# A two-layer encoder on one core: the first feed-forward stage's down projection computed directly, and each stage's opening put in another order

## The chip, the core and the metric

The kernel runs on one core of a Trainium2 chip. The core has five engines that run their own instruction streams and wait for one another by semaphores: TensorE (PE, matmuls; its weight loads are listed apart as PEld), VectorE (DVE), ScalarE (ACT), GpSimd (POOL) and SyncE (SP). POOL and SP issue DMAs too. Matmul operands lie in SBUF, products in eight PSUM banks of 128 x 512 fp32. The metric is the device time of one execution in microseconds; the median of three runs is compared.

## What is computed

The input is 512 prompt tokens and 256 sample tokens, each of width 1024. Both go through the same trunk of two layers (the two batches never mix):

```python
for layer in range(2):
    x = x + 0.5 * swiglu(rms_norm(x, g[layer, 0]), w_gate, w_up, w_down)   # 1024 -> 2816 -> 1024
    hn = rms_norm(x, norm_mix[layer])
    if layer == 0: x = x + concat(s5(u), neighbourhood_attention(q, k, v)) @ w_out_even
    else:          x = x + windowed_gqa(q, k, v) @ w_out_odd
    x = x + 0.5 * swiglu(rms_norm(x, g[layer, 1]), w_gate, w_up, w_down)
return rms_norm(x, norm_final)
```

with `swiglu(x) = (silu(x @ w_gate) * (x @ w_up)) @ w_down`, all in fp32. There are four feed-forward (FFN) stages, q = 0 to 3, and they take most of the time. The S5 mixer of layer 0 is a diagonal state-space scan; it is run in chunks of 8 tokens, for which small matrices (W1, W2, E) are made from its parameters, two of 32 groups at a time.

## The kernel before

*Precision.* Each fp32 operand is split into a rounded high part (ACT's cast, `split`, L89) and a low part (VectorE's subtraction, L90); a product is three matmuls, high x high, high x low, low x high.

*Weights.* One generator, `weights`, fixes the order of all weight tiles. SP loads 128 x 1024 raw blocks into 7 buffers (`raw`, L80); a tile is then split into one of 7 `whl` buffers, four tiles ahead of use (`look`). Where PE is to take a sum of blocks, VectorE forms it in the raw buffers first.

*Gate and up.* The 768 tokens are two halves, 384 each; a pair b takes two of the 22 blocks of the hidden width (11 pairs). Gate and up of a pair each are a 2 x 2 block product computed with seven products instead of eight (Strassen-Winograd): `quad` has steps p1 to p7, one product each of 12 matmuls 128 x 384 (`prod`, L248). The weight sums s1 to s4 are VectorE's (L135 to L141), the token sums t1 to t4 are made once per stage.

*Down.* `down(b)` does the same for the down projection: seven steps of three tiles, 9 matmuls 128 x 512 per step (L354). Of the 21 tiles of results five are added to x by VectorE from PSUM (L358); the other sixteen are scaled into a buffer y by ACT (L361; five buffers) and added to x by an accumulating DMA on POOL's queue (L362). It needs four sums of weights (L114 to L119) and, made in `up`, four sums of h (L330 to L337). `woven` puts one down step after every second product of the next pair. The last pair's down projection is direct (`rows`, L411: 36 matmuls in rows of six) and is not part of this.

*The S5 matrices.* During the first stage, `s5_matrices` runs as a generator, one `next` after each step from b = 2 on. Each of its 16 turns: a chain of small POOL operations (`start`, L626 to L649) into w1, w2; then `finish`: W2d stored by POOL, four transposes of w1 on PE (L660), ACT's copy into w1e, 24 small matmuls on PE (L667 to L671), and two steps later `store`: W1d and Ed by POOL's DMA queue (L678, L679). The next `start` uses w1e as scratch (n1, n2 at L626), so it waits for W1d's DMA.

*A stage's opening.* The tokens' norm and transposes of the last two tiles, the sums t1 to t4 and their splits (`NormS.rest`, a generator: S1 minus S2 at L1263, t3's differences at L1277, the low halves by `lo`, L1226) are interleaved with the products of pairs 0 and 1. The token blocks "22" are held in raw buffers, which loads of weights wait for.

Of the kernel before, what the change touches and what calls it, by code (L numbers as in the profile page):

```python
# [16 lines left out]
ALU = mybir.AluOpType  # L17
# [3 lines left out]
P = 128  # L21
# [26 lines left out]
class Trunk:  # L48
# [49 lines left out]
    def weights(self):  # L98
# [26 lines left out]
        def quad(n, q, b):  # L125

            k = lambda z: (n, q, b, z)
            r1 = self.raw(self.a[n][q, 2 * b])
            a11, a12 = r1[:, :512], r1[:, 512:]
            yield k("11"), self.part(a11)  # L130
            yield k("12"), self.part(a12)
            r2 = self.raw(self.a[n][q, 2 * b + 1])
            a21, a22 = r2[:, :512], r2[:, 512:]
            s1 = self.wp.tile([P, 512], F32, tag="st", name="st", bufs=2)
            v.tensor_add(s1, a21, a22)  # L135
            v.tensor_sub(a21, a11, a21)
            v.tensor_sub(a11, s1, a11)
            yield k("s2"), self.part(a11)
            yield k("s1"), self.part(s1)
            yield k("s3"), self.part(a21)  # L140
            v.tensor_sub(a12, a12, a11)  # L141
            yield k("s4"), self.part(a12)
            yield k("22"), self.part(a22)

        def fast(q):
            both = ("w_gate", "w_up")
            first, second = ([quad(n, q, b) for n in both] for b in range(2))
            for z in first * 2 + second * 2 + first * 5:
                yield next(z)
            for b in range(1, NF // 2):  # L150
                pair = second if b == 1 else [quad(n, q, b) for n in both]
                yield from woven(b, chain(*pair), down(q, b - 1))
            for c in (NF - 2, NF - 1):
                yield from block("w_down", q, c)

# [69 lines left out]
    def ffn(self, q, norm, tail, extra=None):  # L225
# [5 lines left out]
        with ExitStack() as ctx:  # L231
# [5 lines left out]
            extra = extra(fp, room[:, 1, 2:].rearrange("p a n -> p (a n)")) if extra else iter(())  # L237

            def ct():
                return fp.tile([P, H], F32, tag="ct", name="ct", bufs=5)  # L240
# [10 lines left out]
            def quad(n, b, use):  # L251
# [16 lines left out]
                def p2():  # L268
                    o = bank()
                    prod(o, get("12"), "21", True)  # L270
                    v.tensor_add(z["p1"], o, z["p1"])
                    if b != 1:
                        use(0, 0, z["p1"])
# [13 lines left out]

                def p7():
                    prod(z["b"], get("s3"), "t3", False)
                    v.tensor_add(z["r5"], z["b"], z["r5"])  # L290
# [10 lines left out]

                return [p1, p2, p6, p5, p7, p3, p4]

# [6 lines left out]
            def up(b):  # L310

                last = b == NF // 2 - 1
                sums = {}
# [28 lines left out]
            def down(b):  # L342
# [4 lines left out]
                def step(h, w, bank, first, i, j):  # L347
# [19 lines left out]
                    ("s4", "22", "c", False, 0, 1))]  # L367

            def pair(b):
                return quad("w_gate", b, gate), quad("w_up", b, up(b))  # L370
# [4 lines left out]
            rest = norm.rest()  # L375
            for s in (norm.turn, g[0], u[0], norm.turn, g[1], u[1], g1[0], u1[0], g1[1], u1[1]):
                s()
# [6 lines left out]
            for b in range(1, NF // 2):  # L384
                g, u = (z[2:] for z in (g1, u1)) if b == 1 else pair(b)
                for s in woven(b, g + u, iter(down(b - 1))):
                    s()
# [4 lines left out]
            self.warm(at(1, 0)[:, 0:1])  # L392
            act = lambda f, i, n: hs[f"{n // 3 + 1}{f + 1}"][:, i, n % 3 * P : (n % 3 + 1) * P]
            for s in self.rows(act, q, tail):
                s()

    def rows(self, act, q, tail):

        nc = self.nc
        st = {}  # L400

        def step(n):
            t = TILES[n]
            if not st:
                st["t"] = tail()
                st["w"] = [[self.take("w_down", q, c, e) for e in range(2)] for c in (NF - 2, NF - 1)]
            for half in range(2):
                o = self.ps()
                for f, w in enumerate(st["w"]):
                    for j, i in ((0, 0), (1, 0), (0, 1)):  # L410
                        nc.tensor.matmul(o, act(f, i, n), w[half][:, j], start=f == 0 and (j, i) == (0, 0), stop=f == 1 and (j, i) == (0, 1))  # L411
                xs = self.x[t][:, half * 512 : (half + 1) * 512]
                nc.vector.scalar_tensor_tensor(xs, o, 0.5, xs, ALU.mult, ALU.add)
                if half == 0:
                    st["t"].before(t)
            st["t"].after(t)

        return [lambda n=n: step(n) for n in range(6)]

# [45 lines left out]
    def s5_matrices(self, pool, spare):  # L465
# [216 lines left out]
        for q in range(G // 2 + 1):  # L682
            if q:
                finish(q - 1)
                yield
# [524 lines left out]
class NormS(NormT):  # L1210
# [47 lines left out]
    def rest(self):  # L1258
# [3 lines left out]
        for n in range(3):  # L1262
            v.tensor_sub(s1[:, 3 + n], s1[:, 3 + n], s2[:, n])  # L1263
            self.lo("t2", n, s2[:, n])
        yield
        for n in range(3):
            self.lo("t1", n, s1[:, n])
        yield
# [11 lines left out]
        part("22", lambda n: self.C[n])  # L1280
        yield
        part("t4", lambda n: s1[:, 3 + n])
        yield
# [85 lines left out]
```

## Time and profile before

| | |
|---|---|
| runs, median (lowest to highest) | 2759.49 us (2758.82 to 2759.89) |
| the profiled execution | 2754.47 us, span 2752.7 us |
| PE busy | 2624.4 us, 95% of the span |
| DVE, ACT, POOL busy | 2072.1, 1661.6, 919.6 us |
| accumulating DMAs x<-y | 640 issues of 256 KB, 5.2 us to landing in the median |
| S5 stores W1d | 16 issues of 256 KB, 6.1 us in the median |

The span is the time between the first and the last record of that execution. Busy is what an engine's instructions took; matmuls are pipelined, so PE can be busy and still slow when its granted clock is low. The granted clock is given as a share of 2.4 GHz; its other level is 1.2 GHz.

### The profile page before, as it was taken

To read this page: it belongs to the slowest core of one execution; us is meant where nothing else is said; L and a number is where in the kernel's file an instruction comes from. 1 tells how busy PE (TensorE), PEld (TensorE's weight loads), DVE (VectorE), ACT (ScalarE), POOL (GpSimd) and SP (SyncE) were. 2 spreads that over 40 slices of the span, in tenths; PEclk is the share of its full clock that TensorE was granted. 3 is DMA by queue.
4 is the path that set the end of the run, shared out by engine and by line. 5 is a ranking of instruction groups with operands and counts; after the bars stand their busy time and mean duration, and the time that the engine had idled before them with its cause. 6 is when DMAs were issued, how large, how long until landed. Compare 5 with 4: busy or idle time off the path is not lost.

```text
span 2752.7 us, 40909 instructions
## 1 busy us (share of the span) xinstructions
PE 2624.4 (95%) x14276; PEld 2371.8 (86%) x14276; DVE 2072.1 (75%) x3982; ACT 1661.6 (60%) x3432; POOL 919.6 (33%) x1330
## 2 busy tenths in 40 slices
PE   6999999899899989999998999999999999999998
PEld 5987888788778789999997999999897778999997
DVE  7987776664585597787878887878737878787786
ACT  6654554454455566666666666666648766666665
POOL 0378877750380003333331233333200002333332
PEclk8999999899999999999999999999999999999999
DMA  3667676683626128877872778778501116787875
GB/s 140 131 166 155 138 167 138 140 189 96 136 83 180 59 80 192 172 161 162 169 167 66 174 162 172 161 169 169 153 16 55 39 47 155 171 173 170 171 162 132
DMA packets 172271, 381.22 MB, mean 138 GB/s; under 512 B 32960, under 2 KB 39744, under 8 KB 171808
## 3 DMA queue, kind: packets, MB, share of 16 engines
q0 software_dynamic: 96064, 178.89, 36.6%
q1 hardware_dynamic: 76000, 199.72, 23.0%
q8 instruction: 112, 1.84, 0.3%
q14 instruction: 95, 0.78, 0.1%
HBM read 194.97 MB, written 17.89 MB: 77 GB/s over the span
## 4 chain that ended last, share of the span: by engine, by line
PE 78%; POOL 6%; DVE 6%; DMA 5%; ACT 2%; issue 2%; SPq 0%; DVEq 0%; POOLq 0%; ACTq 0%
PE ps L248 39%; PE ps L354 18%; PE ps L222 8%; PE ps L436 4%; DMA W1d<-hct 3%; PE ps L411 2%; POOL x L362 1%; PE ps L1044 1%; DVE whl L90 1%; PE ps L1032 1%; PE ps L1197 1%; DMA x<-y 1%; DMA raw<-in_w_up 1%; PE ps L1063 1%; PE ps L827 1%
## 5 line engine op out<-in xcount | busy, mean ns | idle before, releaser
L362 POOL DMA_DIRECT2D x<-y x640 | 564.3, 1070 | 1166.7 <-ACT y L361 1032.4
L90 DVE TENSOR_TENSOR whl<-raw,whl 128x512 fp32r<-128x512 f32 x876 | 620.1, 713 | 400.3 <-ACT whl L89 388.7
L248 PE MATMUL ps<-bt,whl 128*128 128x384 f32 x4224 | 797.5, 341 | 48.6 <-ACT whl L89 41.0
L248 PEld LDWEIGHTS ps<-bt,whl 128*128 128x128 f32 x4224 | 758.3, 192 | 68.7 <-ACT whl L89 42.7
L89 ACT CAST whl<-raw 128x512 fp32r<-128x512 f32 x876 | 538.7, 620 | 282.3 <-PE ps L248 80.4
L248 PE MATMUL ps<-b,whl 128*128 128x384 f32 x3168 | 593.3, 339 | 1.2 <-DVE hct L317 1.2
L248 PEld LDWEIGHTS ps<-b,whl 128*128 128x128 f32 x3168 | 563.8, 190 | 12.1 <-DVE hct L317 1.6
L361 ACT ACTIVATE y<-ps 128x512 f32<-128x512 f32 x640 | 370.2, 597 | 107.6 <-DMA x<-y 54.5
L354 PE MATMUL ps<-whl,hl 128*128 128x512 f32 x1440 | 361.8, 395 | 0.3 <-ACT y L361 0.3
L354 PEld LDWEIGHTS ps<-whl,hl 128*128 128x128 f32 x1440 | 269.7, 189 | 50.5 <-ACT y L361 0.7
L354 PE MATMUL ps<-whl,h 128*128 128x512 f32 x1080 | 271.9, 395 | 6.4 <-ACT y L361 6.4
L354 PEld LDWEIGHTS ps<-whl,h 128*128 128x128 f32 x1080 | 201.2, 188 | 44.8 <-ACT y L361 8.2
L222 PE MATMUL ps<-hn,whl 128*128 128x256 f32 (+1 forms) x1248 | 229.9, 341 | 0.6 <-ACT hn L89 0.6
L222 PEld LDWEIGHTS ps<-hn,whl 128*128 128x128 f32 x1248 | 192.3, 191 | 29.0 <-issue 2.2
L358 DVE SCALAR_TENSOR_TENSOR x<-ps,x 128x512 f32<-128x512 f32 x200 | 132.8, 682 | 9.8 <-PE ps L354 9.6
L89 ACT CAST h<-hct 128x384 fp32r<-128x384 f32 x132 | 67.9, 514 | 114.5 <-DVE hct L317 114.3
L90 DVE TENSOR_TENSOR whl<-st,whl 128x512 fp32r<-128x512 f32 x128 | 92.1, 723 | 16.1 <-ACT whl L89 14.7
L436 PE MATMUL ps<-whl,ob 128*128 128x512 f32 x432 | 102.8, 392 | 0.0
L286 ACT COPY ct<-ps 128x384 f32<-128x384 f32 x88 | 42.4, 481 | 88.9 <-PE ps L248 88.9
L436 PEld LDWEIGHTS ps<-whl,ob 128*128 128x128 f32 x432 | 80.1, 188 | 18.4 <-issue 1.6
L199 POOL TENSOR_SCALAR ss<-ss 128x1 f32<-128x1 f32 x42 | 13.3, 318 | 243.1 <-ACT raw L198 240.3
L89 ACT CAST whl<-st 128x512 fp32r<-128x512 f32 x128 | 78.5, 617 | 19.3 <-PE ps L248 19.2
(255 smaller groups left out, 3364.7 us busy)
## 6 DMA issues: line engine op xcount, KB each, us to landing
x<-y POOLq DMA_DIRECT2D x640, 256.0 KB, 5.2
raw<-in_w_gate SPq DMA_DIRECT2D x88, 512.0 KB, 5.9
raw<-in_w_up SPq DMA_DIRECT2D x88, 512.0 KB, 3.8
raw<-in_w_down SPq DMA_DIRECT2D x88, 512.0 KB, 5.4
raw<-in_w_in_even SPq DMA_DIRECT2D x16, 512.0 KB, 4.3
raw<-in_w_in_odd SPq DMA_DIRECT2D x10, 512.0 KB, 6.9
W2d<-raw POOLq DMA_DIRECT2D x16, 256.0 KB, 2.4
W1d<-hct POOLq DMA_DIRECT2D x16, 256.0 KB, 6.1
```

The lines of the kernel that those rows point to most:

```text
L89: nc.scalar.copy(hl, src)
L90: nc.vector.tensor_sub(lo, src, hl.bitcast(F32))
L222: self.nc.tensor.matmul(o, w[k // 4][:, j, k % 4 * P : (k % 4 + 1) * P], act[i][k // 4][:, k % 4, k0 : k0 + n], start=k == 0 and (j, i) == ...
L248: nc.tensor.matmul(o, w[:, j, k * P : (k + 1) * P], B[z][:, i, k], start=first and k == 0 and (j, i) == (0, 0), stop=k == 3 and (j, i) == ...
L286: nc.scalar.copy(z["r5"], z["c"])
L354: nc.tensor.matmul(o, hs[h][:, c, n * P : (n + 1) * P], w[:, a], start=first and m == 0, stop=m == 2, skip_group_check=True)
L358: v.scalar_tensor_tensor(xs, o, 0.5, xs, ALU.mult, ALU.add)
L361: nc.scalar.activation(y, o, AF.Copy, scale=0.5)
L362: nc.gpsimd.dma_start(xs, y, accum_op=ALU.add)
L411: nc.tensor.matmul(o, act(f, i, n), w[half][:, j], start=f == 0 and (j, i) == (0, 0), stop=f == 1 and (j, i) == (0, 1))
L436: nc.tensor.matmul(o, act(i, k)[:, t * P : (t + 1) * P], st["w"][k][:, j], start=m == 0, stop=m == 11)
L827: nc.tensor.matmul(o[:, r, e], w1[:, (g2 + e) * 256 + r * P : (g2 + e) * 256 + (r + 1) * P], U[:, 16 * h + b + g2 + e], start=True, stop=True)
```

## The change

Three things are changed. In the first stage (q = 0) the down projection of pairs 0 to 9 is direct, as it was for the last pair alone: `plain`, twelve steps of 6 matmuls 128 x 512, each with one VectorE addition from PSUM into x; the h sums are left out (`last`), the weights are taken as they are, and the order of a pair is seven gate products, twelve short steps, seven up products. The S5 generator gets three more yields in front of `finish`, thirteen per turn. In the opening of every stage the first gate product stands before the norm's turn; p5 (plain sum s1) changes places with p6 (s2) for b = 0, `use(0, 0)` moves to p7; and in `NormS.rest` t1's low halves come first, and S1 minus S2 is put behind "22".

```diff
--- before.py
+++ after.py
@@ -133,14 +133,24 @@
             a21, a22 = r2[:, :512], r2[:, 512:]
             s1 = self.wp.tile([P, 512], F32, tag="st", name="st", bufs=2)
             v.tensor_add(s1, a21, a22)
+            if not b:
+                yield k("s1"), self.part(s1)
             v.tensor_sub(a21, a11, a21)
             v.tensor_sub(a11, s1, a11)
             yield k("s2"), self.part(a11)
-            yield k("s1"), self.part(s1)
+            if b:
+                yield k("s1"), self.part(s1)
             yield k("s3"), self.part(a21)
             v.tensor_sub(a12, a12, a11)
             yield k("s4"), self.part(a12)
             yield k("22"), self.part(a22)
+
+        def plain(q, b):
+
+            r = [self.raw(self.a["w_down"][q, 2 * b + f]) for f in range(2)]
+            for e in range(2):
+                for f in range(2):
+                    yield ("w_down", q, 2 * b + f, e), self.part(r[f][:, e * 512 : (e + 1) * 512])
 
         def fast(q):
             both = ("w_gate", "w_up")
@@ -149,9 +159,11 @@
                 yield next(z)
             for b in range(1, NF // 2):
                 pair = second if b == 1 else [quad(n, q, b) for n in both]
-                yield from woven(b, chain(*pair), down(q, b - 1))
-            for c in (NF - 2, NF - 1):
-                yield from block("w_down", q, c)
+                if q == 0:
+                    yield from chain(pair[0], plain(q, b - 1), pair[1])
+                else:
+                    yield from woven(b, chain(*pair), down(q, b - 1))
+            yield from plain(q, NF // 2 - 1)
 
         def out(n, kb, half):
             for e in range(2):
@@ -236,6 +248,8 @@
             hs = {z: h3[:, i] for i, z in enumerate(("11", "12", "22"))}
             extra = extra(fp, room[:, 1, 2:].rearrange("p a n -> p (a n)")) if extra else iter(())
 
+            act = lambda f, i, n: hs[f"{n // 3 + 1}{f + 1}"][:, i, n % 3 * P : (n % 3 + 1) * P]
+
             def ct():
                 return fp.tile([P, H], F32, tag="ct", name="ct", bufs=5)
 
@@ -269,7 +283,7 @@
                     o = bank()
                     prod(o, get("12"), "21", True)
                     v.tensor_add(z["p1"], o, z["p1"])
-                    if b != 1:
+                    if b > 1:
                         use(0, 0, z["p1"])
 
                 def p6():
@@ -286,6 +300,8 @@
                     nc.scalar.copy(z["r5"], z["c"])
 
                 def p7():
+                    if b == 0:
+                        use(0, 0, z["p1"])
                     prod(z["b"], get("s3"), "t3", False)
                     v.tensor_add(z["r5"], z["b"], z["r5"])
                     use(1, 1, z["r5"])
@@ -299,7 +315,7 @@
                     prod(z["b"], get("22"), "t4", False)
                     use(1, 0, z["b"])
 
-                return [p1, p2, p6, p5, p7, p3, p4]
+                return [p1, p2, p6, p5, p7, p3, p4] if b else [p1, p2, p5, p6, p7, p3, p4]
 
             def gate(f, t, o):
                 nc.scalar.activation(at(f, t), o, AF.Silu)
@@ -309,7 +325,7 @@
 
             def up(b):
 
-                last = b == NF // 2 - 1
+                last = b == NF // 2 - 1 or q == 0
                 sums = {}
 
                 def use(f, t, o):
@@ -366,6 +382,20 @@
                     ("22", "t4", "b", False, 1, 0), ("12", "21", "a", True, 0, 0), ("s1", "t1", "c", True, 1, 1),
                     ("s4", "22", "c", False, 0, 1))]
 
+            def plain(b):
+
+                st = {}
+
+                def step(e, n):
+                    if n == 0:
+                        st["w"] = [self.take("w_down", q, 2 * b + f, e) for f in range(2)]
+                    o = self.ps()
+                    self.rows(o, act, n, st["w"])
+                    xs = self.x[TILES[n]][:, e * 512 : (e + 1) * 512]
+                    v.scalar_tensor_tensor(xs, o, 0.5, xs, ALU.mult, ALU.add)
+
+                return [lambda e=e, n=n: step(e, n) for e in range(2) for n in range(6)]
+
             def pair(b):
                 return quad("w_gate", b, gate), quad("w_up", b, up(b))
 
@@ -373,7 +403,7 @@
             g1, u1 = pair(1)
             self.look = 4
             rest = norm.rest()
-            for s in (norm.turn, g[0], u[0], norm.turn, g[1], u[1], g1[0], u1[0], g1[1], u1[1]):
+            for s in (g[0], norm.turn, u[0], norm.turn, g[1], u[1], g1[0], u1[0], g1[1], u1[1]):
                 s()
             next(rest)
             for z in zip(g[2:], u[2:]):
@@ -383,39 +413,37 @@
                     s()
             for b in range(1, NF // 2):
                 g, u = (z[2:] for z in (g1, u1)) if b == 1 else pair(b)
-                for s in woven(b, g + u, iter(down(b - 1))):
+                for s in g + plain(b - 1) + u if q == 0 else woven(b, g + u, iter(down(b - 1))):
                     s()
                     if b > 1:
                         next(extra, None)
             for _ in extra:
                 pass
...
+    def rows(self, o, act, n, ww):
+
+        for f, w in enumerate(ww):
+            for j, i in ((0, 0), (1, 0), (0, 1)):
+                self.nc.tensor.matmul(o, act(f, i, n), w[:, j], start=f == 0 and (j, i) == (0, 0), stop=f == 1 and (j, i) == (0, 1))
...
@@ -681,6 +709,8 @@
         load(0)
         for q in range(G // 2 + 1):
             if q:
+                for _ in range(3):
+                    yield
                 finish(q - 1)
                 yield
                 yield
@@ -1260,11 +1290,10 @@
         v = self.k.nc.vector
         s1, s2 = self.S
         for n in range(3):
-            v.tensor_sub(s1[:, 3 + n], s1[:, 3 + n], s2[:, n])
+            self.lo("t1", n, s1[:, n])
+        yield
+        for n in range(3):
             self.lo("t2", n, s2[:, n])
-        yield
-        for n in range(3):
-            self.lo("t1", n, s1[:, n])
         yield
 
         def part(z, src):
@@ -1279,6 +1308,8 @@
         yield
         part("22", lambda n: self.C[n])
         yield
+        for n in range(3):
+            v.tensor_sub(s1[:, 3 + n], s1[:, 3 + n], s2[:, n])
         part("t4", lambda n: s1[:, 3 + n])
         yield
```

Three places in the order of instructions. First PE, in the first stage around the first S5 turn, before (ps: PSUM banks; b, bt: token blocks and sums; whl: split weights; h, hl: split hidden values; x9: nine alike in a row):

```order
L248 MATMUL ps<-bt_504,whl 128x384 x12
L248 MATMUL ps<-b_547,whl 128x384 x12
L660 MATMUL ps<-ident,raw 128x128 x4
L667 MATMUL ps<-raw,s5k 32x112 x2
L669 MATMUL ps<-s5k 32x16 x2
L671 MATMUL ps<-raw,s5k 32x112 x2
L667 MATMUL ps<-raw,s5k 32x112 x2
L669 MATMUL ps<-s5k 32x16 x2
L671 MATMUL ps<-raw,s5k 32x112 x2
L354 MATMUL ps<-whl,hl 128x512 x9
L248 MATMUL ps<-bt_598,whl 128x384 x12
```

And after the change, with the new line numbers (L262 product, L446 short step, L688 to L699 the turn):

```order
L262 MATMUL ps<-bt_594,whl 128x384 x12
L446 MATMUL ps<-whl,h_230 128x512 x12
L688 MATMUL ps<-ident,raw 128x128 x4
L695 MATMUL ps<-raw,s5k 32x112 x2
L697 MATMUL ps<-s5k 32x16 x2
L699 MATMUL ps<-raw,s5k 32x112 x2
L695 MATMUL ps<-raw,s5k 32x112 x2
L697 MATMUL ps<-s5k 32x16 x2
L699 MATMUL ps<-raw,s5k 32x112 x2
L446 MATMUL ps<-whl,h_230 128x512 x6
L446 MATMUL ps<-whl,hl 128x512 x3
```

The down steps of nine, one after every second product, have become runs of twelve steps of six behind seven products, and the turn stands behind the second of them; here and at every second turn ten short steps and three products follow it before the next.

POOL in the same stage, from the end of an S5 chain to the next one's beginning, before (hct, raw, s5k: the S5 work's buffers; x<-y: accumulating DMAs):

```order
L648 TENSOR_TENSOR hct<-s5k,raw 128x256
L649 TENSOR_TENSOR raw<-hct 128x2x128
L362 DMA x_82<-y 128x512
L362 DMA x_77<-y 128x512
L362 DMA x_78<-y 128x512
L362 DMA x_79<-y 128x512
L362 DMA x_80<-y 128x512
L678 DMA W1d<-hct 128x512
L612 DMA s5k<-in_s_bc 128x128
L631 TENSOR_SCALAR s5k<-s5k 128x32
L362 DMA x_81<-y 128x512
L679 DMA Ed<-hct 64x240
```

And after:

```order
L676 TENSOR_TENSOR hct<-s5k,raw 128x256
L677 TENSOR_TENSOR raw<-hct 128x2x128
L706 DMA W1d<-hct 128x512
L640 DMA s5k<-in_s_bc 128x128
L659 TENSOR_SCALAR s5k<-s5k 128x32
L707 DMA Ed<-hct 64x240
L654 TENSOR_TENSOR hct<-s5k 128x32
```

The batch of accumulating DMAs between the chain's last instruction and W1d's issue is gone; the S5 work alone is left on POOL.

VectorE in the opening of the second FFN stage, from t3's differences to the first sum of the late weight, before (S1, S2: token sums; bt3, bt4, b22: split token blocks; st: a weight sum):

```order
L1277 TENSOR_TENSOR S2_9535<-raw_9536,S2_9535 128x512
L271 TENSOR_TENSOR hct_9547<-ps_9727,hct_9547 128x384
L1277 TENSOR_TENSOR S2_9535<-raw_9536,S2_9535 128x512
L1277 TENSOR_TENSOR S2_9535<-raw_9619,S2_9535 128x512
L1226 TENSOR_TENSOR bt3_9828<-S2_9535,bt3_9828 128x4x128 x2
L1226 TENSOR_TENSOR b22_9871<-raw_9536,b22_9871 128x4x128
L1226 TENSOR_TENSOR bt3_9828<-S2_9535,bt3_9828 128x4x128
L1226 TENSOR_TENSOR b22_9871<-raw_9536,b22_9871 128x4x128
L1226 TENSOR_TENSOR b22_9871<-raw_9619,b22_9871 128x4x128
L1226 TENSOR_TENSOR bt4_9922<-S1_9418,bt4_9922 128x4x128 x3
L135 TENSOR_TENSOR st_9690<-raw_9688 128x512
```

And after:

```order
L1306 TENSOR_TENSOR S2_8985<-raw_8986,S2_8985 128x512 x2
L285 TENSOR_TENSOR hct_8997<-ps_9171,hct_8997 128x384
L1306 TENSOR_TENSOR S2_8985<-raw_9069,S2_8985 128x512
L1256 TENSOR_TENSOR bt3_9271<-S2_8985,bt3_9271 128x4x128 x2
L333 TENSOR_TENSOR hct_8997<-hct_8997 128x384
L1256 TENSOR_TENSOR bt3_9271<-S2_8985,bt3_9271 128x4x128
L1256 TENSOR_TENSOR b22_9318<-raw_8986,b22_9318 128x4x128
L90 TENSOR_TENSOR h3_8998<-hct_8997,h3_8998 128x384
L1256 TENSOR_TENSOR b22_9318<-raw_8986,b22_9318 128x4x128
L1256 TENSOR_TENSOR b22_9318<-raw_9069,b22_9318 128x4x128
L1312 TENSOR_TENSOR S1_8868<-S1_8868,S2_8985 128x512 x2
L1256 TENSOR_TENSOR bt4_9372<-S1_8868,bt4_9372 128x4x128 x2
L135 TENSOR_TENSOR st_9134<-raw_9132 128x512
```

The three differences of S1 (L1312; before, L1263 in an earlier part of this generator) stand behind the b22 halves, and the steps around them come with other evacuations between.

## Rows read from the trace of the kernel before

**Rows 1.** Windows: start:end, us; busy PE, PEld, DVE, ACT, POOL; clock; DMA; GB/s

```profile
55.73:619.86 564.13, 522.67 (x2819) 473.08 (x2820) 426.19 (x729) 297.59 (x600) 383.45 (x525) 0.94 0.67 153
1003.66:1454.98 451.32, 451.32 (x2371) 423.63 (x2372) 358.82 (x608) 289.10 (x556) 140.27 (x160) 1.00 0.76 165
976.50:997.30 20.80, 17.81 (x106) 17.45 (x104) 20.61 (x37) 15.99 (x32) 0.00 (x0) 1.00 0.13 47
243.29:247.21 3.92, 3.92 (x11) 3.16 (x11) 0.67 (x2) 1.56 (x5) 3.92 (x7) 0.56 1.07 176
```

**Rows 2.** PE's timeline, S5 turns: start, us, instruction, count [idle before <-releaser]

```profile
158.11 0.60 PE L660 MATMUL ps<-ident,raw 128*128 128x128 f32 x4
...
240.85 0.55 PE L660 MATMUL ps<-ident,raw 128*128 128x128 f32 x3 [2.13 <-POOL raw L649]
...
243.29 3.92 PE L354 MATMUL ps<-whl,hl 128*128 128x512 f32 x9
...
265.82 0.60 PE L660 MATMUL ps<-ident,raw 128*128 128x128 f32 x4
...
268.31 2.35 PE L248 MATMUL ps<-bt,whl 128*128 128x384 f32 x12
...
575.31 0.60 PE L660 MATMUL ps<-ident,raw 128*128 128x128 f32 x4
```

**Rows 3.** PE's waits from 56 to 620 us: total us, times, longest

```profile
PE ps L660 <- POOL raw L649: 16.9, 8, 3.8
...
PE ps L354 <- ACT y L361: 6.7, 4, 3.5
```

**Rows 4.** POOL's timeline around one S5 turn

```profile
251.68 0.23 POOL L626 TENSOR_TENSOR hct<-s5k 128x32 f32<-128x32 f32 x1 [1.51 <-DMA W1d<-hct]
...
265.01 4.42 POOL L362 DMA_DIRECT2D x<-y  x5
267.78 2.22 POOL L678 DMA_DIRECT2D W1d<-hct  x1
...
276.47 0.63 POOL L626 TENSOR_TENSOR hct<-s5k 128x32 f32<-128x32 f32 x1 [4.23 <-DMA W1d<-hct]
```

**Rows 5.** The page, section 6: DMA issues, KB each, median us to landing

```profile
W2d<-raw POOLq DMA_DIRECT2D x16, 256.0 KB, 2.4
W1d<-hct POOLq DMA_DIRECT2D x16, 256.0 KB, 6.1
```

**Rows 6.** The chain of waits, its step at the second stage's last rows

```profile
1454.98 8.33 PE ps L411 x36
```

**Rows 7.** PE's timeline, second stage's opening

```profile
1003.66 1.73 PE L248 MATMUL ps<-bt,whl 128*128 128x384 f32 x4 [9.35 <-ACT whl L89]
```

**Rows 8.** SP's timeline there

```profile
997.33 0.33 SPq L80 DMA_DIRECT2D raw<-in_w_up  x1
```

**Rows 9.** VectorE's timeline there

```profile
996.58 1.29 DVE L1226 TENSOR_TENSOR b<-raw,b 128x512 fp32r<-128x512 f32 x2
...
1000.81 0.69 DVE L135 TENSOR_TENSOR st<-raw 128x512 f32<-128x512 f32 x1 [1.14 <-DMA raw<-in_w_up]
...
1002.26 0.69 DVE L137 TENSOR_TENSOR raw<-st,raw 128x512 f32<-128x512 f32 x1
```

**Rows 10.** VectorE's lines, first stage: busy us, mean ns | idle before

```profile
L90 DVE TENSOR_TENSOR whl<-raw,whl 128x512 fp32r<-128x512 f32 x185 | 147.1, 802 | 71.6 <-ACT whl L89 67.8 <-PE ps L354 3.1
L358 DVE SCALAR_TENSOR_TENSOR x<-ps,x 128x512 f32<-128x512 f32 x50 | 33.1, 680 | 5.2 <-PE ps L354 5.2
...
L116 DVE TENSOR_TENSOR raw<-raw,st 128x512 f32<-128x512 f32 x10 | 8.5, 854 | 0.1
```

**Rows 11.** PE's timeline, second stage at its full pace

```profile
1066.28 2.24 PE L248 MATMUL ps<-bt,whl 128*128 128x384 f32 x12
1068.36 2.24 PE L354 MATMUL ps<-whl,hl 128*128 128x512 f32 x9
```

**Rows 12.** VectorE's lines, second stage (1003 to 1455 us)

```profile
L90 DVE TENSOR_TENSOR whl<-raw,whl 128x512 fp32r<-128x512 f32 x189 | 129.6, 688 | 79.4 <-ACT whl L89 77.8
```

More of the change, by code (lines that the diff above doesn't have):

```diff
@@ L392, in ffn, with step @@
             self.warm(at(1, 0)[:, 0:1])
[L393 to L418, printed above, removed]
+            st = {}
+            def step(n):
+                t = TILES[n]
+                if not st:
+                    st["t"] = tail()
+                    st["w"] = [[self.take("w_down", q, c, e) for c in (NF - 2, NF - 1)] for e in range(2)]
+                for half in range(2):
+                    o = self.ps()
+                    self.rows(o, act, n, st["w"][half])
+                    xs = self.x[t][:, half * 512 : (half + 1) * 512]
+                    v.scalar_tensor_tensor(xs, o, 0.5, xs, ALU.mult, ALU.add)
+                    if half == 0:
+                        st["t"].before(t)
+                st["t"].after(t)
+            for n in range(6):
+                step(n)
+    def rows(self, o, act, n, ww):
+        for f, w in enumerate(ww):
+            for j, i in ((0, 0), (1, 0), (0, 1)):
+                self.nc.tensor.matmul(o, act(f, i, n), w[:, j], start=f == 0 and (j, i) == (0, 0), stop=f == 1 and (j, i) == (0, 1))
     def out_pass(self, name, kb, half, act, tail=None):
@@ L1262, in rest @@
         for n in range(3):
-            v.tensor_sub(s1[:, 3 + n], s1[:, 3 + n], s2[:, n])
-            self.lo("t2", n, s2[:, n])
+            self.lo("t1", n, s1[:, n])
         yield
         for n in range(3):
-            self.lo("t1", n, s1[:, n])
+            self.lo("t2", n, s2[:, n])
         yield
```

## The prediction

> **What bounds the kernel now.** I read the page first: PE is busy 95% of the span, and the chain of waits is PE for 78%, so the question is only where PE stands still or runs at its lower clock. The windows answer that by stage. From the end of its opening stall to its last rows the second FFN stage (1003.66 to 1454.98) takes 451.32 us, PE busy all of it, granted clock 1.00; the same stretch of the first stage (55.73 to 619.86) takes 564.13 us, PE busy 522.67, clock 0.94 [rows 1]. Both run the same 145 products of 12 matmuls and 70 down steps of 9. The first has 16 turns of the S5 matrices besides: 28 small matmuls, 2.49 us when nothing is waited for (265.82 to 268.31) [rows 2], 39.8 us in all. So it loses 564.1 - 451.3 - 39.8 = 73.0 us: 41.5 us idle (564.13 - 522.67) and 31.5 us of slow clock.
>
> PE's waits there name causes: POOL's last S5 instruction (L649), 16.9 us in 8 waits, and ACT's evacuation y, 6.7 us [rows 3]; the other 17.9 of the 41.5 us is spread over waits of 3 us and less and one weight that was late. POOL's timeline shows why POOL is late. Its S5 chain, first product (L626, at 251.68) to last (L649, over when the next row begins at 265.01), takes 13.3 us. Then come five issues of accumulating DMAs (L362), 4.42 us, with W1d's issue (267.78) among them; and the next L626, which overwrites what W1d reads, begins at 276.47, 8.7 us after that issue, 4.23 us of them idle for this DMA [rows 4]. W1d lands 6.1 us after its issue in the median, W2d, of the same size but not behind such a batch, 2.4 us [rows 5]. And an idle PE pays twice: after 2.13 us of waiting at 240.85, the next down step took 3.92 us instead of 2.08 (9 of 36 matmuls in 8.33 us) [rows 2, 6]; its window has a clock of 0.56, hence nearly all at 1.2 GHz [rows 1].
>
> The second place is the opening of each FFN stage, where PE idles 9.35 us before 1003.66 for a weight that ACT casts [rows 7]. Read back: the weight is a quad sum, made by three instructions of VectorE, the first at 1000.81 after 1.14 us of waiting for the load of w_up; that load is issued at 997.33 [rows 8], in the middle of VectorE's b22 pair starting at 996.58 [rows 9], when its first half, 0.65 us, has read the raw buffer that the load reuses. The span has four such openings, one for each FFN stage.
>
> **The change, part by part.** *More matmuls.* Per pair the seven down steps (63 matmuls, 7 x 2.08 = 14.6 us) become 72 matmuls, at 8.33/36 = 0.231 us each [rows 6] 16.7 us. Over ten pairs +20.8 us, all on PE, nothing beside it.
>
> *Accumulating DMAs gone in the first stage.* A pair has 21 result tiles, five of which VectorE adds to x at once (50 in ten pairs [rows 10]); sixteen go through ACT and an accumulating DMA. So 160 issues leave POOL's queue, 160 evacuations leave ACT, and PE's 6.7 us for y goes. VectorE gets twelve additions per pair instead of five, 7 x 0.68 = 4.8 us, and loses seven of its weight instructions (four sums, three low halves) and seven of the same kind on h, at 0.80 to 0.85 us the weights [rows 10], those on h, with three quarters of the columns, somewhat less: about -10 us (estimate). It is less loaded than before.
>
> *The S5 turn moves.* A pair now has 26 steps and a turn comes every 13. Between two turns lie, by turns, 11 products and 2 short steps of 6 matmuls (11 x 2.08 + 2 x 1.39 + 2.49 = 28.2 us, eight times; a product takes 2.08 [rows 11]), or 3 products and 10 short steps (22.6 us, seven times). POOL's cycle was 27.8 us on average (158.11 to 575.31, 15 turns) [rows 2]. Now: first transpose to W1d's issue 2.0 us (265.82 to 267.78), landing 3.5, chain 13.3: 18.8 us. Its bounds: 17.7 with W2d's landing of 2.4, and 23.4, the cycle of now less only the 4.42 us of issues. I take 18.8, nearest to W2d's row, since no batch stands ahead of W1d any more. That is under 22.6, so PE's 16.9 us for POOL goes.
> The Trainium skill, DMA: Bandwidth & Descriptors, section Anatomy of one DMA — SWDGE (gpsimd) path, gives 2.0 us and the bytes over 436e3 per us for a DMA of this queue, an estimate of 2.6 us for W1d's 256 KB. W2d's median here agrees with it, W1d's does not; by that page the cycle would be 17.9 us.
>
> *What is left.* Of the 41.5 us idle, 16.9 + 6.7 = 23.6 are the waits named; the others are small lateness of VectorE and ACT, which both lose work. I keep 9 us of the 73 as idle time and slow clock together. Bounds: 0; or 9 and 19 more if the cycle is 23.4, seven waits of 0.8 us (6) and after each the 3.92 - 2.08 = 1.84 us of slow clock (13). First stage: 451.3 + 39.8 + 20.8 + 9 = 520.9, against 564.1: -43.2 us.
>
> *Opening.* Three differences that stood ahead of b22 (the old L1263, 0.64 us each as the b22 halves are [rows 9]) go behind it, so the raw buffer is free some 1.9 us earlier. The first product that waits for the late load is now p5, which takes s1, the plain sum: one VectorE instruction instead of three, 2 x 0.7 less. Together 3.3 us; but the low half of that weight still has VectorE instructions ahead of it, and the third matmul needs it: about -0.5. Each stage gains 2.8 us (bounds: 0 if VectorE reaches b22 no earlier, because it waits for the evacuations before it; 4.5 if the low half is hidden and the clock falls for less time), four stages 11.2. The instructions put later, three differences ahead of t4, lie under the 3.5 us from the load's issue to its first sum [rows 8, 9]. Nothing is removed here.
>
> Sum: -43.2 - 11.2 = -54.4 us. The profiled execution took 2754.47 us (span 2752.7); the median of the runs, 2759.49, is 5.0 above it, and I take the same 54.4 off that: 2705 us.
>
> **Rivals.** *The opening gives nothing.* For it: VectorE is busy 20.61 of the 20.80 us up to 997.30 [rows 1], so moving three instructions helps only if what follows them is ready. Against it: what follows reads loaded weights and old tiles, not PE's newest result. Then 2759.5 - 43.2 = 2716.
>
> *POOL stays the pace.* VectorE's subtractions of two SBUF tiles take 802 ns in the first stage, where POOL is busy 383 us, and 688 ns in the second, where it is busy 140 [rows 1, 10, 12]: the two slow each other, and now the S5 work is packed into less time. If no cycle came under 27.8 us, only the part after the last turn would shrink, from 619.86 - 575.31 - 2.49 = 42.1 us to 7 products and 10 short steps, 28.5: -13.6, and with the openings 2735.
> The Trainium skill, GPSIMD Engine Reference, section Specifications, states that POOL shares its SBUF interfaces with VectorE and contends with instructions that have two SBUF inputs. The trace agrees in the direction; if the chain stretched as those subtractions do, an estimate of 802/688 x 13.3 = 15.5 us, the cycle would be 21.0, still under 22.6, and the sum the same with a margin of 1.6 us.
>
> *VectorE becomes the bound in the short steps.* This one ends slower. For 16.7 us it has to take a tile every 1.39 us, in order, so the weights of the next up products stand behind additions that wait for PE. From (43.2 + 11.2)/10 = 5.4 us of lateness per pair on, all gain is lost; at 8 us 2705 + 80 = 2785. Against it: the additions need only 12 x 0.68 = 8.2 of the 16.7 us, and four weights are made ahead.
>
> *The accumulations were hidden anyway.* Then the loss of 73 us stays under another name: 2759.5 + 20.8 - 11.2 = 2769. The waits for POOL and y [rows 3] speak against it.
>
> **How the numbers follow.** The forecast as a whole 0.56, by itself 2690 to 2715; no gain in the opening 0.20, 2705 to 2725; POOL stays the pace 0.13, 2722 to 2740; slower, by VectorE or hidden anyway, 0.06; no change 0.02; lower still 0.03 (all 73 us and 4.5 us per opening come back: 2759.5 - 52.2 - 18 = 2689, and less if turns gain too). A difference under 0.2% (5.5 us) is about what a measurement of this kernel can't tell from none. Eight in ten: 2686 to 2734. Faster 0.92, same 0.02, slower 0.06.
>
> **What would show it.** The first stage's stretch at 515 to 530 us with a clock of 0.98 or more; waits of the S5 transposes for POOL under 5 us in all; W1d landing in about 3.5 us; from W1d's issue to the next first POOL product under 5 us; opening stalls of 6 to 8 us. Wrong would be: waits for POOL at every second turn, PE waiting for weights after the short steps, or opening stalls as before.

## The result and the profile after

The change made the kernel 2695.82 us (median of 4; before 2759.15), ratio 0.9776 (0.9756 to 0.9796): 63 us, where 54 were forecast. The two profiled executions, on which the rest of this section rests, are 2754.47 and 2695.10 us, spans 2752.7 and 2693.3: 59.4 us apart; the medians differ by 4 us more, and the runs of the kernel before lie between 2754.09 and 2759.89. Cut at the same instructions in both traces, those are: first stage's opening 4.4; its long stretch 42.5 (from the end of the stall to the last product); from its last rows through the first mixer's input products 5.1; the other three openings, each with the stretch behind it, 1.7, 2.5 and 2.8; the rest 0.4.

The windows of the changed kernel (columns as in [rows 1]), the first stage's stretch and the second's:

```profile
51.35:572.80 521.45, 514.96 (x2909) 470.00 (x2910) 378.12 (x665) 192.48 (x383) 217.49 (x365) 0.99 0.26 86
948.74:1400.92 452.18, 452.18 (x2370) 424.31 (x2371) 359.84 (x610) 289.57 (x556) 139.98 (x160) 0.99 0.76 164
```

The first took 564.13 us at a clock of 0.94 [rows 1]. All of PE's waits from 51 to 573 us (the first, 6.1 us, is the opening stall that ends at 51.35), and section 6 of the page:

```profile
PE ps L262 <- ACT whl L89: 6.1, 1, 6.1
PE ps L262 <- ACT ct L294: 3.4, 1, 3.4
PE ps L262 <- ACT hct L280: 2.8, 6, 0.7
```

```profile
W2d<-raw POOLq DMA_DIRECT2D x16, 256.0 KB, 2.4
W1d<-hct POOLq DMA_DIRECT2D x16, 256.0 KB, 2.4
```

No turn waits for POOL [rows 3], and W1d lands like W2d [rows 5]. POOL's timeline around a turn:

```profile
149.60 0.58 POOL L706 DMA_DIRECT2D W1d<-hct  x1 [20.69 <-ACT hct L689]
...
152.13 0.24 POOL L654 TENSOR_TENSOR hct<-s5k 128x32 f32<-128x32 f32 x1 [0.31 <-DMA W1d<-hct]
...
163.73 0.93 POOL L677 TENSOR_TENSOR raw<-hct 128x256 f32<-128x256 f32 x1
```

From W1d's issue to the next chain it is 2.5 us, where it was 8.7 [rows 4], and before that issue POOL now stands idle, waiting for PE and ACT. Over the 15 cycles, from a turn's first transpose to the end of the next chain, the mean is 16.7 us (1.7 to W1d's issue, 3.0 to the chain, 12.0 in it), the longest 20.4; before, the mean was 27.9 (5.75, 6.4, 15.8). The turns stand 22.5 us apart seven times and 28.3 or more eight times, so POOL has time to spare at each.

The opening of the second stage, on PE, SP and VectorE, answering to [rows 7 to 9]:

```profile
948.74 11.43 PE L262 MATMUL ps<-bt,whl 128*128 128x384 f32 x47 [8.76 <-ACT whl L89]
```

```profile
943.66 0.33 SPq L80 DMA_DIRECT2D raw<-in_w_up  x1
```

```profile
924.25 0.68 DVE L1312 TENSOR_TENSOR S<-S,S 128x512 f32<-128x512 f32 x1
...
944.12 1.28 DVE L1312 TENSOR_TENSOR S<-S,S 128x512 f32<-128x512 f32 x2
...
947.35 0.69 DVE L135 TENSOR_TENSOR st<-raw 128x512 f32<-128x512 f32 x1
```

The stall is hardly shorter (8.76 us for 9.35), though each stage gained; the experiments on the opening say why.

### The profile page after: what moved, and what is told of

It is laid out like the page before. It is cut to its first block, busy times and chain, and to the rows that moved or that the text cites. A ratio compares the mean times of both kernels' runs of the same rounds, so it can differ in the third digit from the quotient of the medians.

```text
span 2693.3 us, 40424 instructions
## 1 busy us (share of the span) xinstructions
PE 2614.3 (97%) x14366; PEld 2366.4 (88%) x14366; DVE 2017.2 (75%) x3912; ACT 1555.5 (58%) x3212; POOL 753.2 (28%) x1170
## 3 DMA queue, kind: packets, MB, share of 16 engines
q0 software_dynamic: 73024, 136.94, 28.3%
## 4 chain that ended last, share of the span: by engine, by line
PE 73%; DVE 4%; ACT 2%; DMA 1%; issue 0%; SPq 0%; POOL 0%; DVEq 0%; ACTq 0%; POOLq 0%
PE ps L262 35%; PE ps L370 16%; PE ps L234 8%; PE ps L464 5%; PE ps L446 2%; PE ps L1074 1%; PE ps L1062 1%; PE ps L1093 1%; PE ps L857 1%; DVE raw L222 1%; DVE bt L1256 1%; PE ps L1040 1%; PE ps L829 0%; PE ps L1041 0%; PE ps L793 0%
## 5 line engine op out<-in xcount | busy, mean ns | idle before, releaser
L90 DVE TENSOR_TENSOR whl<-raw,whl 128x512 fp32r<-128x512 f32 x856 | 595.6, 701 | 359.3 <-ACT whl L89 348.4
L262 PE MATMUL ps<-bt,whl 128*128 128x384 f32 x4224 | 789.2, 339 | 39.3 <-ACT whl L89 32.8
L262 PEld LDWEIGHTS ps<-bt,whl 128*128 128x128 f32 x4224 | 750.0, 190 | 58.0 <-ACT whl L89 34.1
L89 ACT CAST whl<-raw 128x512 fp32r<-128x512 f32 x856 | 525.8, 620 | 337.5 <-PE ps L262 83.4
L378 POOL DMA_DIRECT2D x<-y x480 | 421.0, 1033 | 1029.8 <-ACT y L377 841.8
L262 PE MATMUL ps<-b,whl 128*128 128x384 f32 x3168 | 585.7, 336 | 0.2 <-ACT b L1252 0.2
L262 PEld LDWEIGHTS ps<-b,whl 128*128 128x128 f32 x3168 | 556.6, 188 | 8.6 <-ACT b L1252 0.5
L377 ACT ACTIVATE y<-ps 128x512 f32<-128x512 f32 x480 | 280.4, 599 | 47.8 <-PE ps L370 21.6
L370 PE MATMUL ps<-whl,hl 128*128 128x512 f32 x1080 | 269.2, 393 | 0.0
L370 PEld LDWEIGHTS ps<-whl,hl 128*128 128x128 f32 x1080 | 200.9, 188 | 36.5
L370 PE MATMUL ps<-whl,h 128*128 128x512 f32 x810 | 201.9, 393 | 0.0
L446 PE MATMUL ps<-whl,h 128*128 128x512 f32 x756 | 191.1, 392 | 0.0
L370 PEld LDWEIGHTS ps<-whl,h 128*128 128x128 f32 x810 | 150.7, 188 | 27.4
L446 PEld LDWEIGHTS ps<-whl,h 128*128 128x128 f32 x756 | 140.5, 188 | 31.2 <-issue 1.4
L395 DVE SCALAR_TENSOR_TENSOR x<-ps,x 128x512 f32<-128x512 f32 x120 | 81.8, 686 | 43.5 <-PE ps L446 43.2
L90 DVE TENSOR_TENSOR whl<-st,whl 128x512 fp32r<-128x512 f32 x118 | 81.5, 691 | 35.7 <-ACT whl L89 34.4
L374 DVE SCALAR_TENSOR_TENSOR x<-ps,x 128x512 f32<-128x512 f32 x150 | 99.7, 683 | 4.5 <-PE ps L370 4.5
```

The source lines that it names most:

```text
L89: nc.scalar.copy(hl, src)
L90: nc.vector.tensor_sub(lo, src, hl.bitcast(F32))
L262: nc.tensor.matmul(o, w[:, j, k * P : (k + 1) * P], B[z][:, i, k], start=first and k == 0 and (j, i) == (0, 0), stop=k == 3 and (j, i) == ...
L370: nc.tensor.matmul(o, hs[h][:, c, n * P : (n + 1) * P], w[:, a], start=first and m == 0, stop=m == 2, skip_group_check=True)
L374: v.scalar_tensor_tensor(xs, o, 0.5, xs, ALU.mult, ALU.add)
L377: nc.scalar.activation(y, o, AF.Copy, scale=0.5)
```

## Experiments

The theory of the prediction, A: accumulating DMAs on POOL's queue stretch POOL's cycle past the spacing of the turns, and PE waits. Rivals: the turns' new places alone; VectorE's lighter work; a direct product that is cheap in itself. "Stretch" is the first stage from the end of its stall to its last product or rows (0.2 us apart). Ratios are to the kernel before in the same runs.

| kernel | ratio (95%) | stretch, us |
|---|---|---|
| before | 1 | 564.1 |
| the change | 0.9776 (0.9756 to 0.9796) | 521.5 |
| first stage's part alone | 0.9806 (0.9793 to 0.982) | 519.1 |
| opening alone | 0.9957 (0.9941 to 0.9973) | 561.7 |
| change, DMAs back | 0.9814 (0.9798 to 0.9829) | 530.7 |
| change, no yields | 0.9784 (0.9768 to 0.98) | 527.5 |
| change, DMAs back and no yields | 1.0003 (0.9994 to 1.0013) | 582.8 |
| before, one yield | 0.9975 (0.9965 to 0.9984) | 560.2 |
| before, no DMAs | 0.9852 (0.9839 to 0.9866) | 525.2 |

### The two parts alone

The first stage's part with the old opening code, and the old first stage with the new opening.

> The first stage's change alone, with the old opening in all four stages. Theory A (the two parts are independent): the first stage's stretch from the end of its opening stall to its last rows is 521 us as in the changed kernel, opening stalls are 9.4 to 10 us as before, and the whole is 47 to 50 us under the kernel before (42.5 in the stretch, 5 in the rows behind it and the mixer), ratio 0.982. Theory B (the opening's order gives the first stage a lead that lasts): the stretch is 525 us or more and the whole gains 43 us or less.

> The opening's change alone, down projection as before. Theory A: 2 to 3 us in each of four stages, 11 us in all, ratio 0.996; the first stage's long stretch stays at 560 to 566 us. Theory B: where PE waits for POOL afterwards, the first stage gives its lead back, and only three stages gain, 7 us, ratio 0.9975.

Measured: 52 us (2757.66 to 2705.49) and 13 us (to 2744.35) of the medians, 63 for the whole change. In the profiles the long stretch is 519.1 and 561.7 us. Singly they add to 65 us, together they give 63: nearly independent. Theory B of both falls.

### The DMAs back, the yields away, and both

```diff
-                    v.scalar_tensor_tensor(xs, o, 0.5, xs, ALU.mult, ALU.add)
+                    y = fp.tile([P, 512], F32, tag="y", name="y", bufs=5)
+                    nc.scalar.activation(y, o, AF.Copy, scale=0.5)
+                    nc.gpsimd.dma_start(xs, y, accum_op=ALU.add)
...
-                for _ in range(3):
-                    yield
                 finish(q - 1)
```

> The changed kernel, but the twelve tiles of a short-step run go through ACT's scaling and an accumulating DMA on POOL's queue again: 120 issues instead of none, with the direct product, the thirteen steps per turn and the new opening kept. Theory A (the issues on POOL's queue were the loss): W1d lands 5 us or more after its issue, the S5 transposes wait for POOL again, and the first stage takes 25 to 45 us longer than with the change. Theory B (the gain came from the lighter work on VectorE or from the turns' new places): VectorE loses 82 us more of work, and the stage is within 5 us of 521.

> The changed kernel without the three added yields: ten steps per turn as before. Theory A (POOL's cycle is now 15.5 to 18 us, in one case 20.4, and fits any spacing): turns stand 19 to 23 us apart, no wait for POOL but one or two, and the time is within 3 us of the changed kernel, ratio 0.976 to 0.979. Theory B (the yields are what took the waits away): the transposes wait for POOL at every turn in the short steps, 2 to 4 us each with the clock, 15 to 40 us more.

> The changed kernel with both taken back that were taken back singly: the twelve tiles go through ACT and accumulating DMAs (where POOL's cycle was 22.2 us in the mean, 1.0 us under the shorter spacing), and there are ten steps per turn (16 to 24.5 us apart). Theory A (a wait appears only where POOL's cycle is longer than the spacing, so DMAs and yields are each enough): the transposes wait for POOL at more than half of the turns, 15 to 35 us in all, and the stage takes 15 to 40 us longer than with the DMAs back alone. Theory B (the gain is VectorE's lighter work): the two effects add, 11 + 5 us more than the change, ratio 0.983.

With the DMAs back both theories missed: they cost 9 us of the stretch, more than B's 5 and far from A's 25, and no turn waited for POOL. What PE waits for is ACT and VectorE, 14.6 us (with the change 6.2):

```profile
PE ps L262 <- ACT ct L294: 7.8, 2, 7.6
PE ps L262 <- ACT hct L280: 5.1, 7, 1.0
PE ps L262 <- DVE ct L306: 1.7, 1, 1.7
```

```profile
W1d<-hct POOLq DMA_DIRECT2D x16, 256.0 KB, 4.4
```

The mechanism of theory A was there, though: W1d landed after 4.4 us, the cycle rose to 22.2 us (2.6, 4.5, 15.1), and every shorter spacing, 23.4 us here, left 1.0 us. Without the yields theory A held by the ratio: the turns stand 20.7 us apart in the mean, the cycle is 18.8 (15.5 to 18 were expected), and three turns wait:

```profile
PE ps L688 <- POOL raw L677: 3.0, 3, 1.6
```

With both taken back the cycle is 23.3 us, over the 20.7 at which the turns stand without the DMAs. PE's waits are these:

```profile
PE ps L690 <- POOL raw L675: 16.9, 5, 4.8
PE ps L690 <- POOL raw L679: 16.6, 8, 3.0
```

and the windows of the three (DMAs back; no yields; both):

```profile
51.24:581.90 530.66, 516.11 (x2907) 470.76 (x2908) 314.35 (x545) 257.06 (x503) 330.78 (x485) 0.98 0.61 144
```

```profile
52.24:579.77 527.53, 518.92 (x2907) 473.14 (x2908) 379.44 (x665) 193.23 (x383) 229.53 (x365) 0.98 0.27 85
```

```profile
51.48:634.31 582.83, 542.57 (x2907) 488.19 (x2908) 313.65 (x545) 259.91 (x503) 325.95 (x485) 0.93 0.56 131
```

The effects do not add: 9 and 6 us singly, 61 together, 33.5 of it in 13 waits for POOL and 27.6 in more busy time of PE at a clock of 0.93 (542.57 us for the change's 514.96). That is theory A, with 52 us over the DMAs back alone where it said at most 40, and not theory B, which said 16 over the change. The whole kernel is then as slow as before. VectorE has less work in it (314 us) than with the change (378), so its lighter work was not the gain. What decides about these waits is whether POOL's cycle is under the spacing.

### One yield more, without the rest

```diff
             if q:
+                yield
                 finish(q - 1)
```

> The kernel before with one thing changed: one yield more in front of finish, so that eleven instead of ten steps lie between two S5 turns (25.4 us of PE work instead of 23.4, POOL's cycle before being 27.9 us in the mean). Nothing else. Theory A (POOL's cycle is the pace from the first turn to the last, and PE has 20 steps left over behind the last): the cycle stays at 27 to 29 us, 15 steps move from behind the last turn into PE's waits, and the kernel gets 25 to 32 us faster, ratio 0.989 to 0.991, more than half of the change's gain without any of its other parts. Theory C (the cycle follows PE's pace, since both wait for each other): the waits stay as long as they were, within 5 us of the kernel before.

6.6 us (2751.54) instead of 25 to 32: theory A missed, and theory C too, since most of the waits for POOL's last instruction did go, from 16.9 us to 5.7: the turns now stand 29.7 us apart in the mean, and POOL's cycle is 26.4. Others came in their place:

```profile
PE ps L248 <- DVE ct L290: 16.6, 9, 2.9
PE ps L248 <- ACT hct L266: 10.4, 3, 7.7
PE ps L354 <- ACT y L361: 7.1, 6, 2.9
PE ps L660 <- POOL raw L649: 5.7, 2, 4.4
```

ACT's waits in that kernel name a likely source; before, the same line is 45.7 us in 14 waits:

```profile
ACT y L361 <- DMA x<-y: 53.4, 22, 8.8
```

The five buffers y come free only when POOL has issued their DMAs, which stand behind the S5 chain; ACT waits, and so does what is behind it. That the new waits for VectorE come from there is argued from these rows, not tested. So a cycle under the spacing takes away the waits for POOL, and not always the lost time; in this kernel, with its DMAs, one yield gave little. Three were not tried.

### The DMAs gone, without the direct product

```diff
-                        if (i, j) == (1, 0) or (i, j, n) == (0, 0, 0):
+                        if q == 0 or (i, j) == (1, 0) or (i, j, n) == (0, 0, 0):
```

> The kernel before, but in the first stage all 21 tiles of a down step are added to x by VectorE from PSUM: no accumulating DMA in that stage, with the seven-product down projection (no added matmuls), ten steps per turn and the old opening. Theory A: POOL's cycle falls to 17 to 20 us, under the 23.4 us between turns, and the waits for POOL go; but VectorE has 160 x 0.68 = 109 us more on its 426, so it is the bound, and the long stretch takes 515 to 545 us against 564 before and 521 with the change. Theory D (direct computing is cheaper only for VectorE): it takes 564 us or more, VectorE late at every step.

```profile
54.93:580.11 525.18, 499.38 (x2817) 452.64 (x2818) 506.59 (x889) 217.19 (x440) 255.80 (x365) 0.98 0.27 86
```

Theory A held: 38.9 us of the stretch without any direct product, POOL's cycle 21.3 us (a little over the 20 expected, under the 23.4), one wait of 1.0 us for it. One wait of 15.0 us for a weight is left:

```profile
PE ps L248 <- ACT whl L89: 15.0, 1, 15.0
```

I put that down to a small S5 store ahead of a weight load on SP's queue; the run below moved the store to POOL and kept all the rest of this variant, with the last opening of those below:

> The seven-product down projection with all first-stage tiles added by VectorE, with the opening of the run before, and the S5 generator's small store of a8 issued from POOL's queue instead of SP's, where it held back a weight load while PE stood still for 15.0 us. Theory A: 2718 us less 15 (that wait), less 11 and 13 and 8 for the opening's parts, 2671 us, ratio 0.968, level with the direct product: what is saved in matmuls (20.8 us) is lost because VectorE, 506 us of busy time, is the bound of the long stretch at about 510. Theory D (VectorE full means PE waits at every step): 2690 us or more.

0.975 (0.9737 to 0.9764), 2687.91 us, between the two theories: 20 us behind the direct product with the same opening (2667.75, below), and the wait is still there, 15.9 us. My reason was wrong: VectorE's timeline in that wait is full of small S5 instructions, 134.8 to 148.6, and the weight's sum stands behind them:

```profile
134.78 0.18 DVE L540 TENSOR_TENSOR raw<-raw 128x32 f32<-128x32 f32 x1
...
147.97 0.64 DVE L604 COPY raw<-raw 64x512 f32<-64x512 f32 x1
148.63 0.69 DVE L135 TENSOR_TENSOR st<-raw 128x512 f32<-128x512 f32 x1
```

In the kernel before, the same run of small work ends at 138.1, and PE waits 2.6 us behind it (143.68).

### The price of the direct product

`if q == 0` became `if q < 2` at the three places of the change, so the second stage is direct too.

> The changed kernel with the second stage's down projection direct as well. That stage has no S5 work, PE was busy in all of its 452 us and at full clock, so this shows the price of the direct product alone. Theory A: nine more matmuls per pair and 72 x 0.231 - 7 x 2.08 = 2.1 us, the long stretch takes 473 us, the whole 20 to 22 us more than the change. Theory D (less work for VectorE and ACT is worth something by itself): 12 us or less.

```profile
949.44:1416.81 467.37, 467.37 (x2460) 438.57 (x2461) 329.78 (x538) 180.17 (x335) 0.00 (x0) 1.00 0.22 70
```

15.2 us more than the changed kernel's 452.18, between the two theories; the medians say 14.8 (2710.62 us, of two runs). PE is busy throughout in both. A run of 72 takes 16.36 us here (1021.81 to 1038.17), 0.227 us each, not 0.231. Counted from each matmul's start to the next one's, the direct product's 720 take 163.6 us, the 630 that they replace 145.7 in the changed kernel's second stage, so the price is 18 us; the products of 12 took 2.8 us less, part of it fewer slow matmuls behind the opening's stall. Why these were fewer was not tested.

### The opening

The first product ahead of the norm's turn, in the kernel before:

```diff
-            for s in (norm.turn, g[0], u[0], norm.turn, g[1], ...
+            for s in (g[0], norm.turn, u[0], norm.turn, g[1], ...
```

> The kernel before with one move: the first gate product ahead of the norm's turn in each opening. Theory E (VectorE's queue and the load set the stall's end): in stages two to four the 1.9 us wait of the transposes for the norm is filled by that product, but PE only reaches the stall earlier, which grows from 9.4 to 11 us or so; from the last output matmul before a stage to the end of its stall it is 33.2 us as before, within 0.3. Theory G (PE's head start counts): 31.3 us.

```profile
1003.43 1.01 PE L248 MATMUL ps<-bt,whl 128*128 128x384 f32 x2 [11.14 <-ACT whl L89]
```

The stall grew by what PE had won, as theory E has it: from the mixer's last output matmul to the stall's end 33.3 us, before 33.2 (one execution, 2753.96 us in all). In the first stage the stall ends at 54.97 us, with the old opening at 54.93 to 56.03 in four kernels, so nothing is to be seen there either. Then, in the changed kernel, 22's blocks split ahead of t3's low halves, and in a second kernel ahead of t2's as well:

```diff
         yield
-        for n in range(3):
-            self.lo("t2", n, s2[:, n])
-        yield
...
             v.tensor_sub(s2[:, 3 + n], self.C[n], s2[:, 3 + n])
+        part("22", lambda n: self.C[n])
+        for n in range(3):
+            self.lo("t2", n, s2[:, n])
+        yield
         part("t3", lambda n: s2[:, 3 + n])
         yield
-        part("22", lambda n: self.C[n])
         yield
```

This is the second kernel's edit; the first one's moves the line of "22" alone.

> The changed kernel with one more move in every stage's opening: the 22 blocks are split ahead of the low halves of t3, so that the raw buffer that w_up's load waits for is read earlier. Theory E (the stall ends with load, sum, cast in a row): the load is issued 1.8 to 2.8 us earlier, the opening stalls fall from 8.7 to 6.5 us, and the four stages gain 7 to 10 us over the change, ratio 0.973 to 0.975. Theory F (VectorE's queue as a whole, not the place of one instruction in it, sets the end): the first sum comes no earlier, or the low half behind it is later by as much, and nothing is gained, ratio 0.977.

> The changed kernel with the 22 blocks split ahead of t2's low halves too, not only ahead of t3's. Theory E (load, sum, cast in a row end the stall): three more VectorE instructions leave the way of the load, it is issued 1.8 us or more earlier than with the smaller move, that is about when PE runs dry, the stalls fall from 5.8 to about 4 us, and the four stages gain 7 to 9 us more, ratio 0.969. Theory F (t2's low halves are next in need): p6 then waits for t2 as long as p5 waited before, and the time stays at the smaller move's, ratio 0.972.

| second stage's opening, us after the start of the last output matmul | w_up's load issued | stall ends | between |
|---|---|---|---|
| before | 26.9 | 33.2 | 6.3 |
| the change (and the opening alone) | 25.5 | 30.55 | 5.1 |
| 22 before t3 | 22.7 | 27.65 | 4.9 |
| 22 before t3 and t2 | 19.85 | 24.9 | 5.1 |

SP's and PE's rows, in the smaller move and in the last kernel:

```profile
938.06 0.33 SPq L80 DMA_DIRECT2D raw<-in_w_up  x1
```

```profile
942.99 1.33 PE L262 MATMUL ps<-bt,whl 128*128 128x384 f32 x3 [5.85 <-ACT whl L89]
```

```profile
927.25 0.33 SPq L80 DMA_DIRECT2D raw<-in_w_up  x1
```

```profile
932.33 1.95 PE L262 MATMUL ps<-bt,whl 128*128 128x384 f32 x7 [3.13 <-ACT whl L89]
```

2682.69 us, 0.9722 (0.9708 to 0.9735), and 2667.75 us, 0.9677 (0.9664 to 0.9691): theory E both times, with more than it said (13 and 15 us by the medians, 15 and 12 by the ratios, instead of 7 to 10 and 7 to 9). From the load's issue to the stall's end it is 5 us in all three kernels, so the stall ends with the load. The last kernel is the fastest of all here.

## Why the prediction was right

- *Stretch.* 520.9 forecast, 521.45 measured, clock 0.99, no wait for POOL: right. POOL's cycle was 16.7 us, below the lower bound of 17.7: W1d landed after 2.4 us, not the 3.5 that the sum took without a row for it, and the chain fell from 15.8 (the mean; I had taken one turn's 13.3) to 12.0.
- *The cause* was told too simply. The sum put POOL's wait down to the DMAs. With the direct product, DMAs and ten-step spacing are each nearly harmless and together cost 61 us; either edit was nearly enough.
- *More matmuls.* From start to start the first stage's 720 direct matmuls take 164.7 us, the 630 of the second stage 145.7: 19.0 us, not 20.8 (18 by the experiment). The products of 12 take 316.7 us, in the second stage 306.4: what is left of the loss is 10.4 us, not 9. Two small errors cancel, so the half microsecond between 520.9 and 521.45 is in part luck.
- *Opening.* 11.4 us for 11.2, but by other parts: in part luck too. In the second stage the load came 1.4 us earlier, not 1.9: one of the three moved differences still ran early (924.25), two behind b22. From the first sum to the stall's end it is 1.4 us instead of 2.85, one sum instead of three, as the sum had it; 0.2 of that went, since the load took longer to its sum. Of the 2.7 us at the stall's end 1.0 is lost behind it: 19 matmuls run at some 0.32 us, before the change 13. Why is open. The stall of 6 to 8 us did not come in stages two to four because PE reached it 2 us earlier, by the first product ahead of the norm, which by itself is worth nothing. The first stage gained most, 4.4.
- *Not in the sum:* 5.1 us from the first stage's last rows through the first mixer's input products. Before, the transposes behind these rows waited 2.5 us for the norm (630.61), now not; in the products the clock is 0.98 for 0.97. What caused either was not tested.
- *VectorE as bound* did not come true with the direct product (378 us busy); with VectorE at 507 us PE waited 15 us behind a run of its small work.
- *POOL sharing with VectorE:* as a forecast it falls, since no cycle stayed at 27.8 us. Its mechanism is in the rows, though. VectorE's subtractions went from 802 to 749 ns as POOL's busy time went from 383 to 217 us. And POOL's chain, 18 operations and W2d's issue, takes 12.0 us with the change, where VectorE is busy for 75% of it, but 14.3 without the DMAs and without the direct product, where VectorE is busy for 98%. The chain's last operation, with the change and in that run:

```profile
L677 POOL TENSOR_TENSOR raw<-hct 128x256 f32<-128x256 f32 x16 | 13.8, 861 | 1.2
L649 POOL TENSOR_TENSOR raw<-hct 128x256 f32<-128x256 f32 x16 | 17.1, 1067 | 1.3
```

So the chain got shorter by more than the missing DMA issues, and VectorE's lighter work is likely part of it. That is argued from these rows; no run changes VectorE's work alone.

## What to carry to other kernels

Compare a side engine's cycle with the spacing of the points where the main engine needs it: in the changed kernel no wait for POOL was left under it, and over it the waits were paid with slow clock as well, so two edits that each look nearly worthless were worth 61 us together. Look then at what else waits: one yield in the kernel before brought the cycle under the spacing and 6.6 us. Where an engine stands still for a late load, look for what last reads the buffer it reuses and move that read up; a head start for the waiting engine was worth nothing here.

## Not expected of the hardware

Many short waits went with a low clock, the amount of idle time alone did not: the stretch with 13 waits for POOL, 33.5 us, ran at 0.93, the same work with none of them at 0.98, and the run without DMAs, idle for 25.8 us of which 15.0 are one wait, at 0.98 too. POOL's chain of the same 18 operations took 12.0 us with one DMA issue among it, 15.1 with 3.8 in the mean, and 14.3 with one, but beside a VectorE busy for 98% of the time.
